# A chunk by seven block products in the first net too, and a turning without steps

## The chip, the cores and the metric

The kernel runs on one core of a Trainium2 chip. The metric is the device time of one execution in microseconds; the time before is the median of three runs. The span that the profile speaks of runs from the first to the last instruction of one profiled execution.

## The reference

Two layers, each of them a feed-forward net, a mixer (gated convolution, recurrence, pooling), cross attention to a memory, and a second feed-forward net, each followed by a residual and a layer norm. Everything is float32; x and mem are 256 x 1024. What the change touches is the net, which occurs four times (ffn1 and ffn2 of two layers), and the loading of the memory:

```python
D_MODEL = 1024; SEQ = 256; DEPTH = 2; N_MEM = 256; D_FF = 2816

def swiglu(x, w_gate, w_up, w_down):
    return (jax.nn.silu(x @ w_gate) * (x @ w_up)) @ w_down

def reference(x, mem, ...):
    h = x
    for l in range(DEPTH):
        h = layer_norm(ALPHA * h + 0.5 * swiglu(h, ffn1_gate[l], ffn1_up[l], ffn1_down[l]), ...)
        ...                                   # mixer, cross attention with mem
        h = layer_norm(ALPHA * h + 0.5 * swiglu(h, ffn2_gate[l], ffn2_up[l], ffn2_down[l]), ...)
    return h
```

## The kernel before

Every large product is done in three parts: each operand is split into a high part (a float32r copy, made by ScalarE, `whi`, `xTh`, `ah`) and a low part (the rest, a subtraction on VectorE, `wlo`, `xTl`, `al`), and `mm_rows` (L130) issues high x high, high x low and low x high into one PSUM tile. `split` (L60) makes both parts. So each weight that is loaded costs a copy on ScalarE and a subtraction on VectorE for every 128 x 1024 elements.

**Loading.** `load` (L64) brings weights in pieces of 1 MB into `raw` (three buffers) by a DMA on SP's queue, and splits each in two into `whi` and `wlo` (eight buffers each). A load waits until the buffer that it takes over has been split; a split waits until the products of the split eight before it are done.

**A net** (`ffn`, L376) goes over D_FF in chunks of 512 columns (five of them, and a last one of 256). For a chunk, `hidden` (L484) makes gate and up for all 256 tokens (2 weights x 2 token halves x 8 slices of D_MODEL x 3 parts = 96 products of 512 columns), `activate` (L401) and `gated` (L404) form silu(gate) * up in `sg`, and `turn` (L411) brings it to the layout with D_FF on the partitions: four DMAs deal `sg` out into `dealt`, VectorE turns it in 32 x 32 blocks (L418), and the result is split into `ah` and `al`. Down's products (`both`, L631; 24 of them for a slab of 256 rows) follow one chunk later: after chunk c come the second slab of chunk c-2 and the first of chunk c-1.

**A chunk by seven.** Three of the four nets make chunk 3 by `by_seven` (L515) in place of `hidden`. It takes gate and up as the two columns of a 2 x 2 block matrix (the rows being the halves of D_MODEL), x as 2 x 2 blocks (token half by half of D_MODEL), and forms the four result blocks from seven block products instead of eight, after Strassen and Winograd. Sums of x's blocks are made beforehand in `blocks_of_x` (L497: four sums of high and low parts, four combinations, four splits, kept in `kTh` and `kTl`). Sums of weight blocks are made on VectorE in the loaded tiles (L544), and each of the seven weight operands is split afresh: 14 splits. `put` (L565) combines the results. Its weight blocks lie in a tile `spare` (gate's upper half), in the tiles of the layer norm's parameters (`lng`, `lnb`: up's upper half) and in two of the three `raw` buffers.

**The first net** (`early` is set) does not: it also loads the memory (`load_memory`, L179; 32 DMAs on POOL's queue) and some small parameters, turns the memory on VectorE (L195) and splits it into `mTh` and `mTl`, behind chunk 2's work (L654 to L657).

**Order.** The kernel is written against a framework that plans the order of each engine's instructions when the program is built, from its own estimates; `issue_after` and `manual_schedule` steer it. On the chip each engine, and SP's queue of DMAs, then goes through its instructions strictly in that order, waiting at each for what it needs.

The lines that decide which net makes a chunk by seven, and where x's blocks are made:

```python
sevens = (3,) if early is None else ()
...
if c == 1 and sevens:
    bx = blocks_of_x()
```

Of the kernel before, what the change touches and what calls it, by code (L numbers as in the profile page):

```python
# [17 lines left out]
P = 128  # L18
# [28 lines left out]
def model(ctx: ExitStack, tc: tile.TileContext, t: dict, out: bass.AP):  # L47
# [16 lines left out]
    def load(src, k0, nk, c0, ncol, fine=False, strewn=False):  # L64

        hi, lo, todo = [], [], []
        step = 2048 // ncol
        for a in range(k0, k0 + nk, step):  # L70
            raw = wp.tile([P, 2048], F32, tag="raw", name="raw", bufs=3)
            raw = raw.rearrange("p (k c) -> p k c", c=ncol)
            half = step // 2
            part = 1 if fine else step
            for b in range(0, step, part):
                loads.append(nc.sync.dma_start(
                    raw[:, b : b + part, :],
                    src[:, c0 : c0 + ncol].rearrange("(p k) c -> p k c", p=P)[:, a + b : a + b + part, :]
                    if strewn
                    else src[(a + b) * P : (a + b + part) * P, c0 : c0 + ncol].rearrange("(k p) c -> p k c", p=P),  # L80
                ))
# [12 lines left out]
        return Weights(hi, lo, half, todo)  # L94
# [58 lines left out]

    jdn = cst.tile([P, P], F32, name="jdn")
# [24 lines left out]
    def load_memory(mp, behind):  # L179
        m = [mp.tile([P, 4, 8, 32], F32, tag="m", name="m", bufs=2) for _ in range(2)]  # L180
        with tc.issue_after(behind.ins):
            for n in range(2):
                for a in range(4):
                    for k in range(4):
                        c = (4 * n + k) * P + a * 32
                        nc.gpsimd.dma_start(
                            m[n][a * 32 : a * 32 + 32, k],
                            t["mem"][0, :, c : c + 32].rearrange("(b i) j -> i b j", i=32),
                        )

        def later():
            for n in range(2):
                for k in range(0, 4, 2):
                    turned = mp.tile([P, 2, SEQ], F32, tag="up", name="turned")
                    nc.vector.transpose(  # L195
                        turned.rearrange("p k t -> p (k t)"), m[n][:, k : k + 2].rearrange("p k b j -> p (k b j)")
                    )
# [6 lines left out]
    rows = cst.tile([P, P], F32, name="rows")  # L204
# [10 lines left out]
    def small_parameters(op):  # L215
        nc.gpsimd.memset(rows, 0.0)
# [13 lines left out]
        mf = op.tile([P, NT, len(narrow), 64], F32, name="mf", bufs=1)  # L230
# [61 lines left out]
    def finish(mm, y, scale, gb, last=False, flip=False):  # L292
# [6 lines left out]
        for i in range(NT):  # L299
# [8 lines left out]
            for c in pieces:  # L308
# [6 lines left out]
                else:  # L315
                    mm(
                        i, n, slice(0, 512), None,
                        None if last or not i or not n else lambda: transposed(h[0], 0, xTh, xTl),
# [21 lines left out]
        return lambda: transposed(h[1], 1, xTh, xTl, jdn if flip else idn)  # L340

    def project_back(slabs, late, gb, scale, between=lambda: None):
# [30 lines left out]
        return finish(tail, y, scale, gb)  # L373


    def ffn(l, name, n, pend=None, last=False, early=None):  # L376
        gate, up, down = (t[f"{name}_{x}"][l] for x in ("gate", "up", "down"))
        with tc.tile_pool(name="ffn", bufs=2, reuse_waits="tile") as fp:
# [21 lines left out]

            def activate(s, i, og):  # L401
                nc.scalar.activation(halves(s[:, i, :]), sums(og), AF.Silu)

            def gated(s, i, ou):  # L404
                v = halves(s[:, i, :])
                nc.vector.tensor_tensor(v, sums(ou), v, op=ALU.mult)
# [4 lines left out]
            def turn(s):  # L411
# [4 lines left out]
                for i in range(NT):  # L416
                    d = fp.tile([P, 4, P], F32, tag="up", name="square")
                    nc.vector.transpose(  # L418
                        d.rearrange("p k (i b) -> p b k i", b=4), x[:, :, i, :].rearrange("p b (j k) -> p b k j", k=4)
# [4 lines left out]
            def first():  # L424
# [5 lines left out]
                if pend is None:  # L430
# [8 lines left out]
                    with tc.manual_schedule(engines={E.Activation, E.DVE, E.PE}):  # L439
# [8 lines left out]
                        transposed_half(h[0], 0, 0, xTh, xTl)  # L448
                        busy(1)
                        split(*wg.todo[0])  # L450
                        transposed_half(h[0], 0, 1, xTh, xTl)
# [3 lines left out]
                        transposed_half(h[1], 1, 0, xTh, xTl)  # L455
                        group(1, 0)
                        split(*wg.todo[2])
                        transposed_half(h[1], 1, 1, xTh, xTl)
# [38 lines left out]
            def blocks_of_x():  # L497

                d = fp.tile([P, 4, 4 * P], F32, tag="spare", name="quarters", bufs=1)
                q = [d[:, n, :].rearrange("p (k t) -> p k t", t=P) for n in range(4)]  # L500
# [14 lines left out]
            def by_seven(c0, bx):  # L515
                def quarter(m, j, halves_of):
                    for b, r in enumerate(halves_of):
                        n = r.shape[1]
                        k = 4 * j + b * n
                        loads.append(nc.sync.dma_start(  # L520
                            r, m[k * P : (k + n) * P, c0 : c0 + CHUNK].rearrange("(k p) c -> p k c", p=P)
                        ))
                    return [r[:, 2 * h : 2 * h + 2, :] for h in range(2) for r in halves_of[:1]] if n == 4 else halves_of

# [3 lines left out]
                def raw():  # L528
                    return rows_by_columns(wp.tile([P, 2048], F32, tag="raw", name="raw", bufs=3))

                w00 = quarter(gate, 0, [rows_by_columns(
                    fp.tile([P, 4, 4 * P], F32, tag="spare", name="sum", bufs=1).rearrange("p n c -> p (n c)")
                )])
                w01 = quarter(up, 0, [
                    rows_by_columns(wp.tile([P, DM], F32, tag=g, name="raw")) for g in ("lng", "lnb")
                ])
                w11 = quarter(up, 1, [raw()])
                w10 = quarter(gate, 1, [raw()])

                def parts_of(r, plus=None):  # L540
                    hi, lo = [], []
                    for i in range(2):
# [4 lines left out]
                        h, w = (x.rearrange("p (k c) -> p k c", c=CHUNK) for x in (h, w))  # L547
# [14 lines left out]
                def half_sum():  # L562
                    return halves(fp.tile([P, 4, P], F32, tag="up", name="half").rearrange("p k t -> p (k t)"))

                def put(o, a, op, b):  # L565
                    nc.vector.tensor_tensor(o, a, b, op=op)

                s = activations()
                g = [halves(s[:, i, :]) for i in range(NT)]
                o = [acc((P, CHUNK)) for _ in range(4)]  # L570
                run(o[0], part_of_x(0, 0), parts_of(w00))
                nc.scalar.copy(g[0], sums(o[0]))
# [3 lines left out]
                put(e, sums(o[1]), ALU.add, g[0])  # L576
                run(o[3], bx[2], parts_of(w01, w11))
                put(g[1], sums(o[3]), ALU.add, e)
                f = half_sum()
                put(f, sums(o[2]), ALU.subtract, g[1])  # L580
                put(e, sums(o[2]), ALU.subtract, e)
                m = acc((P, CHUNK))
                run(m, part_of_x(0, 1), parts_of(w10))
                put(g[0], sums(m), ALU.add, g[0])
                nc.scalar.activation(g[0], g[0], AF.Silu)
                m = acc((P, CHUNK))
                run(m, part_of_x(1, 1), parts_of(w00, w10))
                put(g[1], sums(m), ALU.add, g[1])
                nc.scalar.activation(g[1], g[1], AF.Silu)
                put(g[1], g[1], ALU.mult, f)  # L590
                m = acc((P, CHUNK))
                run(m, bx[3], parts_of(w11))
                put(e, sums(m), ALU.add, e)
                put(g[0], g[0], ALU.mult, e)
                return turn(s)

            def last_hidden(c0):
# [11 lines left out]
                split(ah[:, 0:2, :], al[:, 0:2, :], s)  # L609
                return ah, al  # L610

            def slab(c, u):
                if c < len(chunks) - 1:
                    w = load(down[c * CHUNK : (c + 1) * CHUNK], 2 * u, 2, 0, DM, strewn=True)
                else:
                    w = load(down, c * 4, 2, 0, DM)
# [4 lines left out]
            sevens = (3,) if early is None else ()  # L621
# [17 lines left out]
            for c, (c0, ncol) in enumerate(chunks):  # L639
# [33 lines left out]
            return finish(tail, ys, 0.5, gb, last=last, flip=name == "ffn1")  # L673
# [27 lines left out]
    def mixer(l, fill):  # L701
        w_in = t["w_in"][l]
        with tc.tile_pool(name="mix", bufs=1, reuse_waits="tile") as mp:
# [284 lines left out]
            return project_back([slab(a) for a in (0, 6, 2, 4)], 3, gb, 1.0)  # L988


    def attention(l, pend):
        scale = (DM // HEADS) ** -0.5
        with tc.tile_pool(name="att", bufs=1, reuse_waits="tile") as ap:
# [108 lines left out]
            return project_back([slab(a) for a in (0, 2, 4, 6)], 3, gb, 1.0, others)  # L1102
# [40 lines left out]
```

## Time and profile before

| | |
|---|---|
| time, median of 3 runs | 1081.91 us (1081.46 to 1082.29) |
| the profiled execution | 1082.44 us, its span 1080.7 us |
| granted TensorE clock | 0.998 |
| PE (TensorE) busy | 1071.4 us, 99% of the span |
| DVE (VectorE) busy | 908.4 us, 84% |
| ACT (ScalarE) busy | 592.8 us, 55% |
| POOL (GpSimd) busy | 61.0 us, 6% |
| DMA | 231.86 MB, mean 215 GB/s |

In the profile's rows, an entry of the timeline is: start, duration, engine, line, operation, output <- inputs, shape, count, and in brackets the idle time just before it and what ended it. An entry of the chain of work that ended last is: start, duration, engine, output tile, line, count. A group's row ends with busy time and mean ns of one, and the idle time before them. The windows give for each stretch its length, then busy time and number of instructions of PE, of its weight loads, of DVE, ACT and POOL, the granted clock, the DMA engines' share and their GB/s. Instructions on an engine overlap a little, so that the step from one start to the next is shorter than the duration of one.

### The profile page before, as it was taken

Reading aid. Unit: us, or ns where it says so; the run is one execution under the profiler, and the core shown is the slowest. Engines: PE = TensorE matmul, PEld = TensorE weight load, DVE = VectorE, ACT = ScalarE, POOL = GpSimd, SP = SyncE. Lnnn points to the kernel's source line nnn. Section 1 sums busy time; section 2 is a strip of 40 time slices with the busy share of each in tenths; the row PEclk is TensorE's granted clock in tenths of the full one; section 3 lists DMA queues with packets and bytes.
Section 4 is the critical chain, followed back from the end, with each engine's and each line's share of the span. In section 5 each row is a group of like instructions: output and inputs, shape, how many; then the busy total and the mean of one; then the engine's idle time right before and its main releaser. Section 6 shows DMA issues by size and latency. Waiting matters only on the chain.

```text
span 1080.7 us, 15689 instructions
## 1 busy us (share of the span) xinstructions
PE 1071.4 (99%) x6015; PEld 947.5 (88%) x6015; DVE 908.4 (84%) x1198; ACT 592.8 (55%) x828; POOL 61.0 (6%) x113
## 2 busy tenths in 40 slices
PE   9999999999999999999999999999999999999997
PEld 7888888989899888888888888898898998888886
DVE  6678677998988898998697998798989889889885
ACT  6456553766457455556365465456764664645650
POOL 9500001000000000000000000010000000000000
PEclk9999999999999999999999999999999999999999
DMA  9986764754476387288468459656536664773761
GB/s 325 289 293 203 249 223 153 237 196 165 167 263 204 123 295 269 96 275 286 156 234 282 166 166 329 229 165 241 174 122 231 240 228 154 255 253 109 260 236 39
DMA packets 122715, 231.86 MB, mean 215 GB/s; under 512 B 6352, under 2 KB 45552, under 8 KB 117520
## 3 DMA queue, kind: packets, MB, share of 16 engines
q1 hardware_dynamic: 120848, 228.48, 63.1%
q0 software_dynamic: 1216, 1.20, 0.4%
q10 hardware_dynamic: 576, 1.18, 0.3%
q8 instruction: 47, 0.77, 0.3%
q14 instruction: 28, 0.23, 0.1%
HBM read 216.15 MB, written 1.05 MB: 201 GB/s over the span
## 4 chain that ended last, share of the span: by engine, by line
PE 99%; DMA 0%; DVE 0%; issue 0%; DVEq 0%
PE acc L106 65%; PE dn L106 30%; PE acc L170 1%; PE dn L845 1%; DMA h<-in_x_dram 0%; PE dn L904 0%; PE dn L903 0%; PE dn L893 0%; PE acc L969 0%; PE dn L810 0%; PE dn L437 0%; DVE h L334 0%; DVE h L330 0%; DVE st L322 0%; DVE h L314 0%
## 5 line engine op out<-in xcount | busy, mean ns | idle before, releaser
L62 DVE TENSOR_TENSOR wlo<-raw,whi 128x1024 fp32r<-128x1024 f32 (+1 forms) x390 | 460.8, 1207 | 91.0 <-ACT whi L61 81.1
L61 ACT CAST whi<-raw 128x1024 fp32r<-128x1024 f32 (+1 forms) x390 | 391.2, 1040 | 258.3 <-PE dn L106 128.4
L106 PE MATMUL acc<-whi,xT 128*128 128x512 f32 x1192 | 359.7, 380 | 0.0
L106 PEld LDWEIGHTS acc<-whi,xT 128*128 128x128 f32 x1192 | 225.2, 189 | 32.1
L106 PE MATMUL acc<-wlo,xT 128*128 128x512 f32 x596 | 225.9, 379 | 0.0
L106 PE MATMUL acc<-xT,whi 128*128 128x512 f32 x576 | 142.1, 382 | 0.0
L106 PE MATMUL dn<-whi,ah 128*128 128x512 f32 x346 | 131.5, 380 | 0.0
L106 PE MATMUL dn<-wlo,ah 128*128 128x512 f32 x346 | 131.2, 379 | 0.0
L106 PE MATMUL dn<-whi,al 128*128 128x512 f32 x346 | 131.1, 379 | 0.0
L106 PEld LDWEIGHTS acc<-wlo,xT 128*128 128x128 f32 x596 | 112.7, 189 | 15.7
L106 PEld LDWEIGHTS acc<-xT,whi 128*128 128x128 f32 x576 | 104.1, 190 | 11.8
L106 PE MATMUL dn<-whi,xT 128*128 128x512 f32 x288 | 88.8, 382 | 0.0
L106 PEld LDWEIGHTS acc<-xT,wlo 128*128 128x128 f32 x576 | 75.5, 191 | 3.9
L106 PE MATMUL acc<-xT,wlo 128*128 128x256 f32 x576 | 75.9, 275 | 0.0
L106 PEld LDWEIGHTS dn<-wlo,ah 128*128 128x128 f32 x346 | 65.4, 189 | 9.5 <-DVE wlo L62 0.3
L106 PEld LDWEIGHTS dn<-whi,al 128*128 128x128 f32 x346 | 65.4, 189 | 9.3
L106 PEld LDWEIGHTS dn<-whi,ah 128*128 128x128 f32 x346 | 65.4, 189 | 9.1
L418 DVE STREAM_TRANSPOSE square<-dealt 128x512 f32<-128x512 f32 x40 | 62.8, 1645 | 3.8 <-DMA dealt<-sg 3.8
L327 POOL TENSOR_TENSOR rs<-rs,nhalf 128x1 f32<-128x1 f32 x16 | 14.9, 928 | 846.3 <-DVE rs L326 846.3
L106 PEld LDWEIGHTS dn<-whi,xT 128*128 128x128 f32 x288 | 54.7, 190 | 7.8 <-DVE xT L62 0.3
L106 PE MATMUL dn<-wlo,xT 128*128 128x512 f32 x144 | 54.8, 381 | 0.0
L61 ACT CAST ah<-square 128x512 fp32r<-128x512 f32 x40 | 24.6, 619 | 39.7 <-DVE square L418 39.7
(227 smaller groups left out, 1174.0 us busy)
## 6 DMA issues: line engine op xcount, KB each, us to landing
raw<-in_ffn_down_dram SPq DMA_DIRECT2D x44, 1024.0 KB, 5.4
raw<-in_ffn_up_dram SPq DMA_DIRECT2D x41, 1024.0 KB, 6.1
raw<-in_ffn_gate_dram SPq DMA_DIRECT2D x39, 1024.0 KB, 5.1
raw<-in_w_in_dram SPq DMA_DIRECT2D x24, 1024.0 KB, 5.0
dealt<-sg SPq DMA_DIRECT2D x80, 128.0 KB, 3.8
raw<-in_ca_k_dram SPq DMA_DIRECT2D x8, 1024.0 KB, 4.9
raw<-in_w_out_dram SPq DMA_DIRECT2D x8, 1024.0 KB, 4.8
raw<-in_ca_v_dram SPq DMA_DIRECT2D x8, 1024.0 KB, 5.4
```

What stands on the lines that cost most here:

```text
L61: nc.scalar.copy(hi, src)
L62: lows.append(nc.vector.tensor_tensor(lo, src, hi.bitcast(F32), op=ALU.subtract))
L106: nc.tensor.matmul(o, w, x, start=start, stop=stop)
L170: nc.tensor.transpose(pt[:, k, :], src[:, (4 * j + k) * P : (4 * j + k + 1) * P], unit)
L327: nc.gpsimd.tensor_tensor(rs, rs, nhalf[:, 0:1], op=ALU.pow)
L418: nc.vector.transpose(d.rearrange("p k (i b) -> p b k i", b=4), x[:, :, i, :].rearrange("p b (j k) -> p b k j", k=4))
L845: nc.tensor.matmul(o[g, hh, :], kc[:, hh, g], x, start=True, stop=True)
```

## The change

1. The first net makes chunk 4 by seven (`sevens = (4,)`). Its `blocks_of_x` is called after the memory's turning has been issued, with c = 2; the layer norm's parameters are loaded only at c = 5, since their tiles hold weight blocks until then.
2. The weight blocks get other tiles. `spare` becomes three tiles of 512 KB. In the first net gate's upper half lies in a whole `raw` buffer, up's lower half in another, gate's lower half in `spare0` and `spare1` (which before that hold the memory and x's blocks); in the other nets gate's upper half in `spare0` and `spare1`, gate's lower half in `dealt` and `spare2`, up's lower half in a `raw` buffer. Every block is loaded by two DMAs of 512 KB.
3. In `by_seven` the product with up's lower half moves ahead of the two with gate's lower half, and the final silu and product go into a second `sg` tile.
4. The turning: `activate` and `gated` write their columns in another order, in two pieces of 256 per token half, and `turn` reads and writes runs of 32 elements in place of steps of four. Down's rows are then loaded in their natural order, the tokens stand in another order in x's layout (a permuted identity `pdn` in the transposes on TensorE for the nets), and the last chunk's activations are split in that order.

Cut to its core, the diff is:

```diff
+    pdn = cst.tile([P, P], F32, name="pdn")
+    nc.gpsimd.tensor_copy(pdn.rearrange("p (r b) -> p b r", b=4), idn.rearrange("p (b r) -> p b r", b=4))
...
     def load_memory(mp, behind):
-        m = [mp.tile([P, 4, 8, 32], F32, tag="m", name="m", bufs=2) for _ in range(2)]
+        m = [
+            mp.tile([P, DM], F32, tag=f"spare{n}", name="m", bufs=1).rearrange("p (k b j) -> p k b j", k=4, j=32)
+            for n in range(2)
+        ]
...
+            def ordered(v):
+                return v.rearrange("p (a k j) -> p k a j", a=4, j=32)
+
+            def by_two(v, o):
+                o = o.rearrange("p (n a j m) -> p m n a j", n=2, a=4, m=2)
+                return [(ordered(v)[:, 2 * m : 2 * m + 2], o[:, m]) for m in range(2)]
+
             def activate(s, i, og):
-                nc.scalar.activation(halves(s[:, i, :]), sums(og), AF.Silu)
+                for v, o in by_two(s[:, i, :], og):
+                    nc.scalar.activation(v, o, AF.Silu)

             def gated(s, i, ou):
-                v = halves(s[:, i, :])
-                nc.vector.tensor_tensor(v, sums(ou), v, op=ALU.mult)
+                for v, o in by_two(s[:, i, :], ou):
+                    nc.vector.tensor_tensor(v, o, v, op=ALU.mult)
...
                     nc.vector.transpose(
-                        d.rearrange("p k (i b) -> p b k i", b=4), x[:, :, i, :].rearrange("p b (j k) -> p b k j", k=4)
+                        d.rearrange("p k (b r) -> p b k r", b=4), x[:, :, i, :].rearrange("p b (k j) -> p b k j", k=4)
                     )
...
             def blocks_of_x():
-                d = fp.tile([P, 4, 4 * P], F32, tag="spare", name="quarters", bufs=1)
+                d = [fp.tile([P, DM], F32, tag=f"spare{n}", name="quarters", bufs=1) for n in range(2)]
...
             def by_seven(c0, bx):
...
-                w00 = quarter(gate, 0, [rows_by_columns(fp.tile([P, 4, 4 * P], F32, tag="spare", ...))])
-                w01 = quarter(up, 0, [rows_by_columns(wp.tile([P, DM], F32, tag=g, ...)) for g in ("lng", "lnb")])
-                w11 = quarter(up, 1, [raw()])
-                w10 = quarter(gate, 1, [raw()])
+                w00 = block(gate, 0, pieces("spare0", "spare1") if early is None else whole())
+                w01 = block(up, 0, pieces("lng", "lnb"))
+                w11 = block(up, 1, whole())
+                w10 = block(gate, 1, pieces("dealt", "spare2") if early is None else pieces("spare0", "spare1"))
...
                 put(e, o[2], ALU.subtract, e)
+                o = [acc((P, CHUNK)) for _ in range(3)]
+                run(o[0], bx[3], parts_of(w11))
+                put(e, o[0], ALU.add, e)
+                run(o[1], part_of_x(0, 1), parts_of(w10))
+                put(g[0], o[1], ALU.add, g[0])
+                run(o[2], part_of_x(1, 1), parts_of(w00, w10))
+                put(g[1], o[2], ALU.add, g[1])
+                s = fp.tile([P, NT, CHUNK], F32, tag="spare2", name="sg", bufs=1)
+                for i, u in enumerate((e, f)):
+                    v = ordered(s[:, i, :])
+                    nc.scalar.activation(v, g[i].rearrange(...), AF.Silu)
+                    nc.vector.tensor_tensor(v, v, u.rearrange(...), op=ALU.mult)
                 return turn(s)
...
-            sevens = (3,) if early is None else ()
+            sevens = (3,) if early is None else (4,)
...
-                if c == 1 and sevens:
+                if sevens and c == 1 and early is None:
                     bx = blocks_of_x()
                 if c == (max(sevens) + 1 if sevens else 1):
-                    with tc.issue_after(loads[-1].ins) if early is not None else nullcontext():
-                        gb = ln_params(l, n)
-                        rest = early(fp) if early is not None else ()
+                    gb = ln_params(l, n)
+                if c == 1 and early is not None:
+                    with tc.issue_after(loads[-1].ins):
+                        rest = early(fp)
                 if c == 2 and early is not None:
                     with tc.issue_after(lows[-1].ins):
                         for f in rest:
                             f()
+                    if sevens:
+                        bx = blocks_of_x()
```

More of the change, by code (lines that the diff above doesn't have):

```diff
@@ L317, in finish @@
                         i, n, slice(0, 512), None,
-                        None if last or not i or not n else lambda: transposed(h[0], 0, xTh, xTl),
+                        None if last or not i or not n else lambda: transposed(h[0], 0, xTh, xTl, units[0]),
                     )
@@ L515, in by_seven, with whole, pieces, block @@
             def by_seven(c0, bx):
[L516 to L523, printed above, removed]
                 def rows_by_columns(r):
                     return r.rearrange("p (k c) -> p k c", c=CHUNK)
[L528 to L536, printed above, removed]
-                w11 = quarter(up, 1, [raw()])
-                w10 = quarter(gate, 1, [raw()])
+                def whole():
+                    r = rows_by_columns(wp.tile([P, 2048], F32, tag="raw", name="raw", bufs=3))
+                    return [r[:, 0:2, :], r[:, 2:4, :]]
+                def pieces(*tags):
+                    pools = {"lng": wp, "lnb": wp}
+                    return [
+                        rows_by_columns(pools.get(g, fp).tile([P, DM], F32, tag=g, name="raw", bufs=1)) for g in tags
+                    ]
+                def block(m, j, to):
+                    for i in range(2):
+                        k = 4 * j + 2 * i
+                        loads.append(nc.sync.dma_start(
+                            to[i], m[k * P : (k + 2) * P, c0 : c0 + CHUNK].rearrange("(k p) c -> p k c", p=P)
+                        ))
+                    return to
+                w00 = block(gate, 0, pieces("spare0", "spare1") if early is None else whole())
+                w01 = block(up, 0, pieces("lng", "lnb"))
+                w11 = block(up, 1, whole())
+                w10 = block(gate, 1, pieces("dealt", "spare2") if early is None else pieces("spare0", "spare1"))
                 def parts_of(r, plus=None):
@@ L671, in tail @@
                         rows_of(a, i, k, m, first, u == 2 and k == 1, cols, alone)
[L673 removed]
+            return finish(tail, ys, 0.5, gb, (idn, jdn) if name == "ffn1" else (pdn, pdn), last=last)
     def keys(l, c, between={}):
```

77 lines of the change are left out of this document (33 added, 44 removed).

## Prediction

> **What bounds the kernel now.** I read the page's first part, then the chain of work that ended last in order of time, then the windows and the timeline of VectorE around the stretches that the diff touches.
>
> ```profile
> span 1080.7 us, 15689 instructions
> PE 1071.4 (99%) x6015; PEld 947.5 (88%) x6015; DVE 908.4 (84%) x1198; ACT 592.8 (55%) x828; POOL 61.0 (6%) x113
> 19.78 31.08 PE acc L106 x144
> ...
> 87.23 20.72 PE acc L106 x96
> 107.95 10.36 PE dn L106 x48
> 118.31 20.72 PE acc L106 x96
> 139.03 10.36 PE dn L106 x48
> ...
> 450.92 18.13 PE acc L106 x84
> ...
> 639.45 10.56 PE dn L106 x48
> ```
>
> TensorE is the bound: the chain is matmuls nearly from end to end. 20.72 / 96 = 0.2158 us from one 512-column product to the next, and 84 x 0.2158 = 18.13: the chunk by seven in the second net runs without a gap. The one excess I see is 0.20 us at 639.45. So only two things count: fewer matmuls, and whether TensorE still finds its operands.
>
> **Part by part: the products.** The plain chunk at 118.31 (the fifth, c = 4) has 96 products; by seven it has 7 x 4 x 3 = 84. 12 x 0.2158 = 2.59 us go, all on the path. Everything else in the diff is off the path as long as it arrives in time.
>
> **The feeding of that chunk.** A product needs the weight's high part (ScalarE) and low part (VectorE). A chunk by seven needs 14 splits in place of 8, 8 sums of weight blocks, 7 combinations of results, and x's four blocks (12 operations) beforehand.
>
> ```profile
> core 0: us, PE busy (x) PEld busy (x) DVE busy (x) ACT busy (x) POOL busy (x), PEclk, DMA share, GB/s
> 86.00:108.00 22.00, 22.00 (x103) 19.27 (x102) 21.09 (x37) 16.07 (x20) 0.00 (x0) 1.00 0.53 185
> 110.00:150.00 40.00, 40.00 (x187) 35.04 (x186) 26.18 (x24) 18.59 (x21) 0.00 (x0) 1.00 0.73 238
> 440.00:480.00 40.00, 40.00 (x187) 35.04 (x186) 39.29 (x41) 22.28 (x25) 0.00 (x0) 1.00 0.49 156
> ```
>
> Where a chunk is made by seven today (440 to 480) VectorE works 39.29 of 40 us. In the first net it has room from 110 to 150 (26.18), but none just before: from 86 to 108, where the memory is turned, 21.09 of 22. The change queues x's blocks exactly there. What today's chunk by seven has that the new one lacks is a head start:
>
> ```profile
> 433.95 1.23 DVE L62 TENSOR_TENSOR wlo<-sum,whi 128x1024 fp32r<-128x1024 f32 x1 [0.93 <-ACT whi L61]
> ...
> 440.01 0.68 DVE L406 TENSOR_TENSOR sg<-acc,sg 128x512 f32<-128x512 f32 x1
> 440.61 1.22 DVE L62 TENSOR_TENSOR wlo<-sum,whi 128x1024 fp32r<-128x1024 f32 x1
> 441.74 0.68 DVE L406 TENSOR_TENSOR sg<-acc,sg 128x512 f32<-128x512 f32 x1
> 442.34 1.22 DVE L62 TENSOR_TENSOR wlo<-sum,whi 128x1024 fp32r<-128x1024 f32 x1
> 443.48 2.35 DVE L544 TENSOR_TENSOR sum<-sum,raw 128x1024 f32<-128x1024 f32 x2
> 445.75 1.22 DVE L544 TENSOR_TENSOR raw<-raw 128x1024 f32<-128x1024 f32 x1
> ...
> 455.51 1.27 DVE L62 TENSOR_TENSOR al<-square,ah 128x512 fp32r<-128x512 f32 x2
> 456.71 3.48 DVE L62 TENSOR_TENSOR wlo<-raw,whi 128x1024 fp32r<-128x1024 f32 x3
> ...
> 468.78 1.20 DVE L62 TENSOR_TENSOR wlo<-raw,whi 128x1024 fp32r<-128x1024 f32 x1
> ```
>
> Splits for the chunk that starts at 450.92 begin at 433.95, before the previous chunk's L406 has its results (440.01, 441.74); in today's order three splits and three sums stand ahead of the second L406. Even so the lead is small: the split of 468.78 ends at 469.98 and its product stands at about 470.4. In the changed program's instruction order the first net's DVE queue holds, after the memory's turning: x's blocks between four down splits, then the four halves of the previous chunk's gating, and only behind them the first of the fourteen splits. The engine runs in order, so no part of that work starts before the previous chunk's last product, 107.95.
>
> **The sum on VectorE.** Start to start a 128x1024 operation takes (445.75 - 443.48) / 2 = 1.135 us and a 128x512 one (456.71 - 455.51) / 2 = 0.60.
>
> ```profile
> 86.20 3.17 DVE L418 STREAM_TRANSPOSE square<-dealt 128x512 f32<-128x512 f32 x2 [1.74 <-DMA dealt<-sg]
> 89.26 1.17 DVE L62 TENSOR_TENSOR wlo<-raw,whi 128x1024 fp32r<-128x1024 f32 x1
> 90.36 1.27 DVE L62 TENSOR_TENSOR al<-square,ah 128x512 fp32r<-128x512 f32 x2
> 91.56 0.17 DVE L260 COPY prm<-acc 128x32 f32<-128x32 f32 x1
> ...
> 92.01 0.69 DVE L195 STREAM_TRANSPOSE turned<-m 128x512 f32<-128x512 f32 x1
> ...
> L418 DVE STREAM_TRANSPOSE square<-dealt 128x512 f32<-128x512 f32 x40 | 62.8, 1645 | 3.8 <-DMA dealt<-sg 3.8
> L1054 DVE STREAM_TRANSPOSE square<-dealt 128x512 f32<-128x512 f32 x6 | 4.2, 705 | 0.0
> L127 DVE TENSOR_TENSOR sums<-acc,sums 128x256 f32<-128x256 f32 x32 | 13.3, 419 | 2.5 <-ACT sums L126 2.5
> ```
>
> The turning without steps has no row of its own; its ends are L418 (1645 ns, steps of four on both sides) and L1054 (705 ns, runs of 32, the shape that the new one has). I take L1054's, 0.62 start to start: 0.87 saved on each. A gating half is bounded by L127 (419 ns): 0.34 start to start.
>
> From 86.20, in the new order: 2 turnings (1.25), 6 splits (6.8), 2 splits of the activations (1.2), the memory's 4 turnings (2.5) and 4 splits (2.4), fifteen small ones at (92.01 - 91.56) / 4 = 0.11 (1.7), x's 12 (7.2): 23.1, so to 109.3, then 4 gating halves (1.4): 110.7. From there to the last of the fourteen splits: 14 splits and 8 sums, 22 x 1.135 = 25.0, and eleven of 0.60 (two turnings, two activation splits, six combinations, one product of silu), 6.6: 142.3. TensorE wants that split after 13 x 6 products and one more: 118.31 + 79 x 0.2158 = 135.4. Two down products stand ahead of it in the new order (0.43). TensorE loses 142.3 - 135.8 = 6.5 us, in several waits.
>
> **Behind it, one more wait.** In the first net the block that is added to (w00) lies in one of the three raw buffers until that last sum is split. The next down load but one needs that buffer, and stands in SP's queue behind the previous chunk's dealing and the norm's two loads, ahead of the sixth chunk's gate and up loads.
>
> ```profile
> raw<-in_ffn_down_dram SPq DMA_DIRECT2D x44, 1024.0 KB, 5.4
> 117.10 1.06 ACT L61 CAST whi<-raw 128x1024 fp32r<-128x1024 f32 x1 [2.88 <-DVE square L418]
> ```
>
> 142.3 + 5.4 + 1.06 = 148.8 for its high part, 149.9 for the low one. TensorE has 5 products of the chunk and 22 down ones left, 27 x 0.2158 = 5.8, and stands there at 148.1: waits of 0.7 and 0.9, and some 0.2 at the second half. I take 1.8. After that the loads follow close on each other, and VectorE is back in its 26 of 40 us.
>
> Sum: -2.59 + 6.5 + 1.8 = +5.7. The profiled execution took 1082.44 (span 1080.7 and 1.74 around it), 0.5 above the median of 1081.91; on the median it gives 1087.6. Bounds: if VectorE is free at 107.95, 1.7 less, and a landing of 4.4 in place of 5.4 takes off 1.0: +3.0, 1084.9. If the turning stays at L418's price, two pairs lie in the sum above: 4 x 0.87 = +3.5, 1091.1.
>
> [...]
>
> **What I cost at nothing.** In the other three nets the split order keeps the early start (three splits ahead of the gating), and the turning inside the stretch is 2 x 0.87 shorter: the 0.4 us lead grows. Splitting activations and gating in two adds 0.34 x 2 - 0.60 = 0.08 on VectorE each, hidden by the same. The permuted identity is one more POOL copy, and the order of tokens changes no matmul. The last chunk's activations are split in two pieces with steps, four times in all, where VectorE has room; down's rows are loaded as w_out's are today. The blocks' loads now come as 512 KB pairs.
>
> ```profile
> 7.05 5.98 SPq L76 DMA_DIRECT2D raw<-in_ffn_up_dram  x2
> 17.60 1.99 ACT L61 CAST whi<-raw 128x1024 fp32r<-128x1024 f32 x2 [0.87 <-DMA raw<-in_ffn_up_dram]
> 18.69 2.40 DVE L62 TENSOR_TENSOR wlo<-raw,whi 128x1024 fp32r<-128x1024 f32 x2 [0.47 <-ACT whi L61]
> 5.00:10.00 5.00, 5.00 (x22) 4.15 (x21) 2.57 (x4) 2.69 (x6) 4.80 (x11) 1.00 1.05 388
> 10.00:15.00 5.00, 5.00 (x26) 4.23 (x25) 4.87 (x8) 4.04 (x9) 5.00 (x11) 1.00 1.02 337
> ```
>
> One of them moves far: up's block of the fifth chunk (lng, lnb) is issued between the first chunk's two up loads, where the DMA engines are full. 1 MB at 388 to 337 GB/s delays the second up load by 2.7 to 3.1 us. Its first low part is ready at 18.69 + 1.2 = 19.9 and wanted at 19.78 + 25 x 0.2158 = 25.2: 5.3 of cover, 2.2 left. If that cover were gone, the delay would be paid in full.
>
> **Rivals.** (a) VectorE keeps up and only the 2.59 count: 1079.3. It decides if the chain above is 7 us shorter, that is, if the splits start before 107.95. For it: today's three chunks by seven lose nothing. Against: the order. 7%. (b) The starvation is there but half as long, because combinations and products overlap better than I count: 1081.91 - 2.59 + 4.2 = 1083.5. 10%. (c) The start starves as well, by the full 3.1 us: 1090.7. 5%. (d) The clock falls in the starved stretch:
>
> ```profile
> 7.03 0.85 PE dn L437 x2
> ```
>
> at the start two products take 0.85, half speed. If the 27 products behind the longest wait ran so, that is 5.8 more: 1093.4. 4%, since the waits come in pieces of about 2 us with products between. [...] (e) My forecast: 74%.
>
> **Numbers.** 1087.6. The range takes in (b)'s upper part, the bounds and (c): 1083.9 to 1091.1; (a) and (d) are left out. No change means within 0.2%, 2.2 us, about what a measurement of this kernel can tell: faster is (a), 0.07; same is the lower part of (b), 0.06; slower 0.87.
>
> **What would show it.** Right: 84 products in the first net's fifth chunk, with waits of PE on wlo and whi of 5 to 9 us in all between about 128 and 150; VectorE without idle from 90 to 150; first split after both gatings; a down load issued only behind the last sum. Turning rows near 705 ns. The other nets' chunks by seven at 18.13. Wrong: an unbroken 18.13 there, or waits before 30 us.

## The result, and the profile after

The changed kernel takes 1087.2 us, the median of four runs (1086.23 to 1087.89), against 1081.68 before: a ratio of 1.0049, 95% interval 1.0032 to 1.0067. Six more runs of it, made beside the experiments, gave 1087.88 and a ratio of 1.0057 (1.0044 to 1.0069). It is slower, by what was forecast to within half a microsecond. The time was lost where the prediction put it, but one term of the sum did not occur, and several smaller losses that the sum did not have came in its place.

The profiled execution took 1086.68 us, its span 1084.9. First the chain of work that ended last, in order of time (start, duration, engine, output tile, line, count; the product line L106 is now L103, the sums of weight blocks L544 are L562, the combinations in `put` are L584, the gating L406 is L420, the turning L418 is L433):

```profile
19.22 31.08 PE acc L103 x144
...
86.67 20.72 PE acc L103 x96
107.39 10.36 PE dn L103 x48
117.75 6.42 PE acc L103 x30
124.18 1.14 DVE wlo L62
125.31 2.27 DVE raw L562 x2
127.58 0.60 DVE half L584
128.18 1.15 DVE wlo L62
...
129.37 8.23 PE acc L103 x29
...
138.31 1.14 DVE raw L562
...
140.51 1.05 ACT whi L61
...
141.60 0.70 PE dn L103 x2
142.30 1.08 PE acc L103 x5
143.38 9.93 PE dn L103 x46
...
163.79 18.37 PE dn L103 x84
...
455.07 18.13 PE acc L103 x84
```

But for one hole, this is TensorE nearly from end to end, as before. The first net's fifth chunk begins at 117.75. Its 84 products and the two down products among them would take 86 x 0.2158 = 18.56 and end at 136.31; the remaining 46 down products begin at 143.38. That is 7.07 us of starvation. From 124.18 to 129.33, and again from 137.62 until ScalarE's last copies, the chain runs over VectorE: splits, sums of weight blocks, combinations. The 8.23 us of TensorE between them are 29 products, which would take 29 x 0.2158 = 6.26; the granted clock had fallen there (see rival (d) below). In the other nets the chunk by seven still takes 18.13.

VectorE's timeline there (start, duration, engine, line, operation, output <- inputs, shapes, count, idle time before it and what ended that):

```profile
107.29 0.68 DVE L62 TENSOR_TENSOR kTl<-quarters,kTh 128x512 fp32r<-128x512 f32 x1
107.89 1.41 DVE L420 TENSOR_TENSOR sg<-acc,sg 128x256 f32<-128x256 f32 x4
109.22 2.35 DVE L62 TENSOR_TENSOR wlo<-raw,whi 128x1024 fp32r<-128x1024 f32 x2
111.49 3.49 DVE L562 TENSOR_TENSOR raw<-raw 128x1024 f32<-128x1024 f32 x3
...
137.62 0.69 DVE L584 TENSOR_TENSOR sg<-acc,sg 128x512 f32<-128x512 f32 x1 [0.24 <-PE acc L103]
...
140.63 3.50 DVE L62 TENSOR_TENSOR wlo<-raw,whi 128x1024 fp32r<-128x1024 f32 x3 [0.59 <-ACT whi L61]
```

The last of x's blocks is split just before the four gating halves (L420), and the first of the chunk's fourteen splits starts at 109.22, behind them. The windows say the same:

```profile
core 0: us, PE busy (x) PEld busy (x) DVE busy (x) ACT busy (x) POOL busy (x), PEclk, DMA share, GB/s
86.00:108.00 22.00, 22.00 (x104) 19.26 (x103) 21.51 (x44) 16.77 (x25) 0.00 (x0) 1.00 0.44 152
108.00:142.00 34.00, 30.14 (x127) 24.44 (x126) 33.17 (x38) 15.53 (x18) 0.00 (x0) 0.95 0.43 129
```

VectorE is busy for 33.17 of 34 us while TensorE falls to 30.14 and ScalarE to 15.53. ScalarE is named by some of TensorE's waits (acc waits 3.1 us for whi), but it has half of that stretch free: it waits for VectorE's sums itself, 13.3 us in four waits of `whi` on `raw`.

### The profile page after: what moved, and what is told of

It reads as the page before. It is cut to its first block, busy times and chain, and to the rows that moved or that the text cites. A ratio compares the mean times of both kernels' runs of the same rounds, so it can differ in the third digit from the quotient of the medians.

```text
span 1084.9 us, 15815 instructions
## 1 busy us (share of the span) xinstructions
PE 1071.5 (99%) x6003; PEld 945.5 (87%) x6003; DVE 906.4 (84%) x1267; ACT 606.8 (56%) x875; POOL 62.3 (6%) x114
## 4 chain that ended last, share of the span: by engine, by line
PE 98%; DVE 1%; DMA 0%; issue 0%; ACT 0%; DVEq 0%; SPq 0%; ACTq 0%
PE acc L103 65%; PE dn L103 30%; PE acc L170 1%; PE dn L866 1%; DMA raw<-in_ffn_gate_dram 0%; PE dn L925 0%; DVE raw L562 0%; DVE wlo L62 0%; PE dn L914 0%; PE dn L924 0%; ACT whi L61 0%; PE acc L990 0%; PE dn L831 0%; DVE h L338 0%; DVE h L334 0%
## 5 line engine op out<-in xcount | busy, mean ns | idle before, releaser
L62 DVE TENSOR_TENSOR wlo<-raw,whi 128x1024 fp32r<-128x1024 f32 (+1 forms) x420 | 496.6, 1208 | 105.5 <-ACT whi L61 96.8
L61 ACT CAST whi<-raw 128x1024 fp32r<-128x1024 f32 (+1 forms) x420 | 421.4, 1042 | 277.4 <-PE dn L103 114.1
L103 PE MATMUL acc<-whi,xT 128*128 128x512 f32 x1152 | 348.7, 380 | 1.9 <-ACT whi L61 1.9
L103 PEld LDWEIGHTS acc<-whi,xT 128*128 128x128 f32 x1152 | 217.7, 189 | 33.2 <-ACT whi L61 2.3
L103 PE MATMUL acc<-wlo,xT 128*128 128x512 f32 x576 | 218.4, 379 | 0.0
L103 PE MATMUL acc<-xT,whi 128*128 128x512 f32 x576 | 142.1, 382 | 0.0
L103 PE MATMUL dn<-whi,ah 128*128 128x512 f32 x346 | 131.4, 380 | 0.5 <-ACT whi L61 0.5
L103 PE MATMUL dn<-wlo,ah 128*128 128x512 f32 x346 | 131.2, 379 | 0.0
L103 PE MATMUL dn<-whi,al 128*128 128x512 f32 x346 | 131.1, 379 | 0.0
L103 PEld LDWEIGHTS acc<-wlo,xT 128*128 128x128 f32 x576 | 108.9, 189 | 15.5 <-DVE wlo L62 0.3
L103 PEld LDWEIGHTS acc<-xT,whi 128*128 128x128 f32 x576 | 104.1, 190 | 11.8
L103 PE MATMUL dn<-whi,xT 128*128 128x512 f32 x288 | 88.3, 381 | 0.0
L103 PEld LDWEIGHTS acc<-xT,wlo 128*128 128x128 f32 x576 | 75.5, 191 | 3.9
L103 PE MATMUL acc<-xT,wlo 128*128 128x256 f32 x576 | 75.9, 275 | 0.0
L103 PEld LDWEIGHTS dn<-whi,ah 128*128 128x128 f32 x346 | 65.3, 189 | 9.9 <-ACT whi L61 0.8
L103 PEld LDWEIGHTS dn<-wlo,ah 128*128 128x128 f32 x346 | 65.4, 189 | 9.7 <-DVE wlo L62 0.4
L103 PEld LDWEIGHTS dn<-whi,al 128*128 128x128 f32 x346 | 65.4, 189 | 9.2
L103 PEld LDWEIGHTS dn<-whi,xT 128*128 128x128 f32 x288 | 54.4, 189 | 7.6 <-DVE xT L62 0.2
L103 PE MATMUL dn<-wlo,xT 128*128 128x512 f32 x144 | 54.8, 380 | 0.0
L324 DVE SCALAR_TENSOR_TENSOR h<-h,dn 128x512 f32<-128x512 f32 x31 | 21.1, 682 | 27.3 <-PE dn L103 27.3
L103 PE MATMUL acc<-whi,mT 128*128 128x512 f32 x128 | 40.2, 380 | 0.0
```

Of the source, the lines that this page charges most:

```text
L61: nc.scalar.copy(hi, src)
L62: lows.append(nc.vector.tensor_tensor(lo, src, hi.bitcast(F32), op=ALU.subtract))
L103: nc.tensor.matmul(o, w, x, start=start, stop=stop)
L324: nc.vector.scalar_tensor_tensor(v, v, ALPHA / scale, sums(y[i][n]), op0=ALU.mult, op1=ALU.add)
```

## The experiments

The theory after the result: VectorE, in order and without idle time from 87 us on, is the bound of the first net's chunk; x's blocks beside the memory's turning take the time in which the chunk's splits would have run ahead. The rivals: something else of the change costs (the turning, the tiles, the loads), ScalarE or the loads are what is late, or the clock.

**Only the first net back to plain chunks.**

```diff
-            sevens = (3,) if early is None else (4,)
+            sevens = (3,) if early is None else ()
```

> The changed kernel, but the first net makes all its chunks plainly again: the turning without steps, the other tiles and the other three nets' sevens stay. VectorE's lateness in the first net's seven-product chunk as the whole loss: 1081.1 us (1080.4 to 1081.9), as before less the 0.56 us by which the chunk begins earlier. If the turning, the tiles or the other nets cost: 1084 to 1087.

Measured: 1081.51 us, ratio 1.0001 (0.9992 to 1.0010). Together, the turning, the tiles and the other nets' new order cost and bring nothing; the whole loss is the one chunk. The 0.56 us of earlier start that the expectation counted as a gain was none: the profiled execution of before had a span of 1080.7, while most of its other runs (1079.7 to 1080.5) and this kernel have 1079.8.

**x's blocks earlier.** They are made with c = 1, in the two tiles `lng` and `lnb` that are free then.

```diff
             def blocks_of_x():
-                d = [fp.tile([P, DM], F32, tag=f"spare{n}", ...) for n in range(2)]
+                d = [fp.tile(... tag=f"spare{n}" ...) if early is None else wp.tile(... tag=("lng", "lnb")[n] ...) for n in range(2)]
...
-                if sevens and c == 1 and early is None:
-                    bx = blocks_of_x()
+                if sevens and c == 1:
+                    with tc.issue_after(loads[-1].ins) if early is not None else nullcontext():
+                        bx = blocks_of_x()
...
-                    if sevens:
-                        bx = blocks_of_x()
```

> x's blocks of the first net are made behind its second chunk, in the two normalization tiles, and not beside the memory's turning; nothing else is moved by hand. VectorE's queue ahead of the chunk as the cause: 12 instructions, 7.2 us, leave the stretch from 86 us on, VectorE's last split falls from 142 to about 135 us, which is when TensorE wants it; 1078.3 to 1079.8 us, faster than both kernels. If VectorE's work within the chunk (38 us by its own rows) is the cause and not what stands ahead: 1083 to 1086. If ScalarE's roundings or the loads are what is late: 1086 to 1087, as the changed kernel.

Measured: 1079.55 us (1079.48 to 1081.05), ratio 0.9982 (0.9974 to 0.9991). This version beats both kernels, and in its chain the chunk by seven is unbroken:

```profile
117.63 18.13 PE acc L103 x84
```

With the blocks gone the planner filled the place with the chunk's own work, as VectorE's timeline shows:

```profile
102.44 2.49 DVE L567 TENSOR_TENSOR raw<-raw 128x1024 f32<-128x1024 f32 x2
104.84 1.22 DVE L62 TENSOR_TENSOR wlo<-raw,whi 128x1024 fp32r<-128x1024 f32 x1
106.10 1.23 DVE L567 TENSOR_TENSOR raw<-raw 128x1024 f32<-128x1024 f32 x1
107.24 0.75 DVE L420 TENSOR_TENSOR sg<-acc,sg 128x256 f32<-128x256 f32 x2
```

Sums of weight blocks (L567 here) now stand ahead of the gating. Its windows show how near the edge it is: TensorE whole, VectorE 37.56 of 38.

```profile
86.00:108.00 22.00, 22.00 (x104) 19.26 (x103) 20.97 (x39) 16.09 (x23) 0.00 (x0) 1.00 0.68 232
108.00:146.00 38.00, 38.00 (x178) 33.28 (x177) 37.56 (x41) 22.96 (x26) 0.00 (x0) 1.00 0.55 167
```

**No sums of weight blocks in the first net.**

```diff
-                        if plus is not None:
+                        if plus is not None and early is None:
                             nc.vector.tensor_tensor(r[i], r[i], plus[i], op=ALU.add)
```

> The changed kernel without the eight sums of weight blocks in the first net's chunk (left out; the seven products use the blocks unsummed). VectorE as the bound: 8 times 1.14 = 9.1 us less in the chunk, last split at 133 us, ahead of TensorE's want: 1078.3 to 1079.8 us. If ScalarE's roundings or the loads are late, of which nothing is taken away: 1085 to 1087. If the clock's fall makes the loss: 1083 to 1085.

Measured: 1079.24 us, ratio 0.9980 (0.9971 to 0.9989). This kernel leaves the sums out of what it computes, and nothing else. Taking work from VectorE alone, with every copy of ScalarE's and every load kept, removes the whole loss. ScalarE and the loads fall as rivals. So does the clock: with the splits held behind the gating and with the steps back (both below) the loss stands, and the profiled clock is 1.00 throughout the chunk.

**x's blocks twice over.** The call of `blocks_of_x` for the first net is repeated.

> The changed kernel, x's blocks of the first net made twice over: 12 instructions, 7.2 us, more for VectorE in the stretch in which it has no idle time. VectorE as the bound of that stretch: 7.2 us longer, and up to 2 more where the last chunk's loads come late behind it: 1094.4 to 1096.5. If TensorE, ScalarE or the loads share the bound there, less than 5 us: under 1092.

Measured: 1096.68 us (1095.33 to 1100.32), ratio 1.0143 (1.0128 to 1.0158): 9 us more than the changed kernel for 7.2 us more of VectorE, shortest against shortest (1095.33 and 1086.23); the median lies just above the range that was expected. The profiled run, the longest, is no measure of the blocks alone. It lost 4.7 us before they were made: its chain has the 96 products that start at 55.48 in the changed kernel at 60.16, behind loads that took longer to land (up's 1 MB from 10 to 52 us 9.6 us in the median, in the changed kernel 7.2). And its granted clock was 0.87 from 108 to 142 us:

```profile
133.00:143.00 10.00, 8.47 (x19) 5.77 (x19) 9.45 (x9) 7.67 (x8) 0.00 (x0) 0.50 0.19 68
```

**The order alone.** Two kernels that differ in one thing. In both, x's blocks are queued behind the second chunk's last split; in the second, each split of the chunk is also queued behind the gating.

```diff
-                    with tc.issue_after(loads[-1].ins) if early is not None else nullcontext():
+                    with tc.issue_after(lows[-1].ins) if early is not None else nullcontext():
                         bx = blocks_of_x()
```

> As with x's blocks early, but held behind the last split of the second chunk, so that all twelve instructions lie between 65 and 87 us, still ahead of the memory's turning. VectorE's work ahead of the chunk as the cause: that they leave the stretch from 87 us on decides and not where they go, 1079.0 to 1079.8 us. If their place in VectorE's early gaps mattered: 1081 to 1083.

```diff
+                    gates.append(nc.vector.tensor_tensor(v, o, v, op=ALU.mult))
...
-                        split(h, w, r[i])
+                        with tc.issue_after(gates[-1].ins) if early is not None else nullcontext():
+                            split(h, w, r[i])
```

> The kernel with x's blocks held behind the second chunk's last split, and in the first net's seven-product chunk each split queued behind the previous chunk's four gating halves, as the changed kernel has them. The amount of work is that of the faster kernel, the order that of the slower. If the order is half of the cause: VectorE idles from about 102 us (86.2 plus 23.1 less 7.2) until the gating's product at 107.4, some 5.3 us, less the splits of the down block that may go ahead, 3.4; 2 to 5 us lost: 1081.5 to 1084.5. If the amount alone decides: 1079.0 to 1079.8. If the order alone decides: 1086 to 1087.

Measured: 1081.31 us (1079.54 to 1083.45; ratio 0.9995, 0.9986 to 1.0003) and 1086.77 us (1084.95 to 1087.44; ratio 1.0042, 1.0030 to 1.0055). The first missed its expectation: where the blocks go does matter, by 1.8 us in the median. Put in one lump they delay the third chunk's gating and with it the dealing and the loads; in its chain a load of up's block stands at 100.58 for 4.70 us. VectorE's turning there starts at 87.25 after 3.51 us of waiting for the dealing, where with the blocks early it was 84.64 and 0.93. The second lost more than expected. Its VectorE:

```profile
89.37 1.30 DVE L433 STREAM_TRANSPOSE square<-dealt 128x512 f32<-128x512 f32 x2 [5.43 <-DMA dealt<-sg]
...
101.41 3.57 DVE L62 TENSOR_TENSOR wlo<-raw,whi 128x1024 fp32r<-128x1024 f32 x3
106.01 0.76 DVE L420 TENSOR_TENSOR sg<-acc,sg 128x256 f32<-128x256 f32 x2 [1.03 <-PE acc L103]
107.31 0.76 DVE L420 TENSOR_TENSOR sg<-acc,sg 128x256 f32<-128x256 f32 x2 [0.54 <-PE acc L103]
107.98 2.35 DVE L62 TENSOR_TENSOR wlo<-raw,whi 128x1024 fp32r<-128x1024 f32 x2
```

VectorE stands idle in front of the gating with splits behind it, and the first one starts at 107.98, hardly earlier than the changed kernel's 109.22. Part of the time that the blocks left went idle sooner, in the 5.43 us of waiting for the dealing. That wait is 1.9 us longer than in the first kernel's profile, ahead of the place where the two differ; but since VectorE still waits for TensorE's products at the gating (1.03 and 0.54 us), it is not what held the chunk's splits up. The order costs 5.5 us between the medians of these two. So both halves are needed: the blocks must leave, and the time that they leave must be filled with the chunk's work.

**x's sums on GpSimd.** In `blocks_of_x`, `nc.gpsimd.tensor_tensor` in place of `nc.vector.tensor_tensor` in the first net.

> The changed kernel, the eight sums and differences of x's blocks of the first net made by GpSimd, which is idle from 50 us on; their four splits stay on VectorE, and the planner then puts splits and sums of the chunk ahead of two of the gating halves. VectorE's work ahead of the chunk and its order as the cause: 8 times 0.6 = 4.8 us less, filled with the chunk's own splits, last split at 137.5 instead of 142.3 us where TensorE wants it at 136; 1080.5 to 1082.5 us. If freed time is not filled, as where the splits stand behind the gating: 1084 to 1086. If GpSimd is late with them or slows VectorE: 1087 or more.

Measured: 1089.33 us, ratio 1.0071 (1.0057 to 1.0084), no faster than the changed kernel and in the median slower (the intervals overlap), although the planner ordered the chunk's splits ahead of the gating. VectorE's timeline while GpSimd works:

```profile
90.70 3.41 DVE L62 TENSOR_TENSOR wlo<-raw,whi 128x1024 fp32r<-128x1024 f32 x2
94.03 1.23 DVE L277 TENSOR_TENSOR s<-e 128x4 f32<-128x4 f32 x1
...
103.08 4.51 DVE L62 TENSOR_TENSOR wlo<-raw,whi 128x1024 fp32r<-128x1024 f32 x2
```

and the groups of GpSimd (name, shapes, count, busy us, mean ns):

```profile
L518 POOL TENSOR_TENSOR quarters<-xT 128x512 f32<-128x512 f32 x4 | 7.8, 1955 | 42.9 <-DVE turned L198 40.8 <-DVE lbs L283 2.1
```

Two splits take 3.41 and 4.51 us where two take 2.35 without GpSimd, and an operation of 4 columns takes 1.23. VectorE's busy time from 86 to 108 us was 21.66 us with 32 instructions, against 21.51 with 44 in the changed kernel: what was moved away came back as longer instructions. What holds VectorE up there the trace does not name.

GpSimd was late as well. The chain runs over its sums, and the last one stands there at 106.58:

```profile
99.14 3.47 POOL quarters L518 x2
...
106.58 2.15 POOL quarters L526
```

ScalarE's copy of that sum, at 108.76, has the last three pieces of the gating's silu behind it, and the gating on VectorE starts at 116.86 in place of 107.89. How much each of the two costs was not separated.

**The turning in steps again**, in the changed kernel and in the faster one.

```diff
-                        d.rearrange("p k (b r) -> p b k r", b=4), x[:, :, i, :].rearrange("p b (k j) -> p b k j", k=4)
+                        d.rearrange("p k (i b) -> p b k i", b=4), x[:, :, i, :].rearrange("p b (j k) -> p b k j", k=4)
```

> The changed kernel, its turning of a chunk read and written in steps again (this leaves the columns of a chunk in another order, so the order is what is left out). VectorE late in one chunk of the first net only: the two turnings in the stretch without idle cost 0.94 us more each, 1.9 in all: 1089.1 us (1088.3 to 1090.3); the other nets' turnings cost nothing. If the turning has no part in it: 1087.2. If every net pays: over 1092.

> The kernel with x's blocks behind the second chunk and each chunk's turning in steps again (which leaves the columns of a chunk in another order). VectorE at its edge in every net's seven-product chunk: the first net, full from 87 to 146 us but for 1.1 us, loses 1 to 3 us, the three others 1.3 each as they did with the steps in the changed kernel: 1084.5 to 1086.5 us. If the steps cost only where VectorE is already late: 1079.5 to 1080.5.

Measured: 1094.43 us (ratio 1.0117, 1.0103 to 1.0131) and 1085.38 us (ratio 1.0039, 1.0026 to 1.0051). The rows of the turning, in the changed kernel and then with steps:

```profile
L433 DVE STREAM_TRANSPOSE square<-dealt 128x512 f32<-128x512 f32 x40 | 26.0, 687 | 1.5 <-DMA dealt<-sg 1.5
```

```profile
L433 DVE STREAM_TRANSPOSE square<-dealt 128x512 f32<-128x512 f32 x40 | 62.7, 1646 | 7.3 <-DMA dealt<-sg 7.2
```

The first expectation missed, by 5 us, and its rival, that every net pays, came true. Set mark against mark along the two chains, the first net loses 2.9 us (1.9 were expected), and each of the three others 1.4, which I had held to be free. In the faster kernel the three lose 1.35 each again and the first net 1.8, which was foretold once the first miss was known. So the turning without steps gives no time of its own, but all four chunks by seven stand on it in this order of instructions: in the three other nets two turnings in the stretch are 1.9 us, and only some 0.5 of that was spare.

**Two chunks by seven in each of the other nets**, on top of the blocks behind the second chunk:

```diff
-            sevens = (3,) if early is None else (4,)
+            sevens = (2, 4) if early is None else (4,)
```

> As with x's blocks held behind the second chunk's last split, and the other three nets make two chunks each, the third and the fifth, by seven products. TensorE alone: 36 products fewer, 7.8 us, 1071.5 us. With VectorE as the second bound: one such chunk keeps it busy for 26.5 of 28 us and the stretch ahead of it for 26.4 of 31, and in these nets the third chunk comes right behind the making of x's blocks, so that it starves as the first net's did, 4 to 7 us in each net: 1083 to 1093.

Measured: 1099.30 us, ratio 1.0169 (1.0154 to 1.0184). TensorE has 36 products fewer and the kernel is 18 us slower than the one it builds on: VectorE is busy for 61.83 of 63 us from 378 to 441, and the waits come in all three nets: 0.8 to 1.2 us in the third chunk (437.66 in the second net), and 3.1 to 3.5 us in the fifth (498.43 to 503.18 there). The direction was foretold, the size was not.

## Why the prediction was right, point by point

- **The products.** 84 in the chunk, 2.59 us fewer on TensorE: the chain of the kernel with early blocks has the chunk in an unbroken 18.13, and its span is 2.3 us shorter than the plain one's (1079.8 to 1077.5; the time 1.96, 1081.51 to 1079.55). Right.
- **VectorE is late because the splits stand behind gating and blocks.** Right in mechanism and nearly in its marks: first split 109.22 (predicted 110.7); the last is the first of the three that start at 140.63 and ends at about 141.8 (142.3); starvation 7.07 (6.5). The queue ahead was ready 1.4 us sooner than summed, 1.0 of it since the stretch's first turning ran at 83.75 and not at 86.20; two waits of VectorE, 0.24 and 0.59, gave part of that back. One sign came out smaller than named: the waits that the profile names for TensorE from 127 to 142 us are 3.86 us in all (0.76, 0.46, 0.31, 1.87, 0.46) and not 5 to 9. The rest of the 7.07 is TensorE at the lower clock, 1.7, and the slower start of products behind each wait (the first takes 0.48 us, where the step from one to the next is 0.2158).
- **"Behind it, one more wait", 1.8 us.** This step failed. SP's queue:

```profile
131.61 0.38 SPq L75 DMA_DIRECT2D raw<-in_ffn_down_dram  x1
141.89 0.38 SPq L75 DMA_DIRECT2D raw<-in_ffn_gate_dram  x1
```

  The down load went out at 131.61, before the last sum (138.31 in the chain); it took over another raw buffer. The load that waited for the summed block's buffer is the next chunk's gate (141.89, as that block's last split ends), whose products come 46 down products later. Behind 143.38 the chain has 0.24 us too much (18.37 at 163.79). I had not followed which of the three buffers each load takes. With the stepped turning such a wait does appear: there the chain stands for 8.31 us on a load of the sixth chunk's up block that starts at 146.25.
- **The sum.** 7.07 - 2.59 = 4.48, 0.16 by a later start than in the plain kernel (19.22 against 19.06) and 0.24 behind it: 4.88 of the 5.1 by which this span exceeds 1079.8. So the forecast +5.7 met the measured +5.5 of the medians in part by luck. The 1.8 did not occur; 0.6 more of starvation, the 0.16 and the 0.24 made up for half of it in this execution; in the other traced one the clock added 1.7, next.
- **Rival (d), the clock.** It was given 4% and held unlikely since the waits would come in pieces of about 2 us. That such waits leave the clock whole was an estimate of mine; here it fell behind waits of 0.76 us and less. The row at 7.03 from which the half speed was taken shows no fall: the granted clock there is 1.00 (7.03 to 7.88 us in the profile of before). TensorE's timeline, and a window of the same stretch:

```profile
126.49 0.38 PE L103 MATMUL acc<-whi,kTl 128*128 128x512 f32 x1
127.63 0.48 PE L103 MATMUL acc<-whi,kTh 128*128 128x512 f32 x1 [0.76 <-ACT whi L61]
128.58 0.48 PE L103 MATMUL acc<-whi,kTh 128*128 128x512 f32 x1 [0.46 <-ACT whi L61]
129.37 0.48 PE L103 MATMUL acc<-wlo,kTh 128*128 128x512 f32 x1 [0.31 <-DVE wlo L62]
...
131.14 0.63 PE L103 MATMUL acc<-whi,xT 128*128 128x512 f32 x1
131.56 0.63 PE L103 MATMUL acc<-wlo,kTh 128*128 128x512 f32 x1
...
131.00:133.00 2.00, 2.00 (x6) 1.55 (x6) 2.00 (x3) 1.32 (x2) 0.00 (x0) 0.50 0.70 193
```

  Three waits under a microsecond with two products between them, three more products at full speed, and then eight that stand 0.43 us apart, until 133.3. In this execution that cost next to nothing: VectorE was the bound, and waited 0.24 us for a product. In the profiled execution of the second set the clock held through that stretch and fell behind the last waits, 1.54 and 0.46 us:

```profile
141.00:143.00 2.00, 1.96 (x7) 1.61 (x8) 0.72 0.21 24
143.00:145.00 2.00, 2.00 (x6) 1.64 (x5) 0.50 1.00 341
145.00:147.00 2.00, 2.00 (x10) 1.69 (x10) 0.93 1.09 387
```

  (PE, its weight loads, the clock, the DMA engines' share, GB/s.) There TensorE is the bound again, and from 141.04 on it took 1.7 us more than the first execution for the same products; that run took 1087.95 us. So the ten runs' scatter, 1086.2 to 1089.4, may be in part where the clock falls; I have that from two traces only. The second set was made to see whether the runs with the lower mean clock are the longer ones. The two shortest of the ten do have the highest (0.999 and 0.998), but the other eight, 1086.68 to 1089.37, all show 0.996 or 0.997, so that it is not shown. Nor do the traces show what makes the clock fall. The price of (d), 5.8 us, was too high for these two executions: in both the clock was at half for 3.4 us, which is 1.7 us of lost work. That is no limit: with the blocks made twice the clock stayed at half for 10.2 us, from 133.0 to 143.2.
- **Rivals (a), (b), (c).** (a) and (b) fell by the 7.07. (c): TensorE has no wait between the start and 124 us, so the hoisted load stayed inside its cover.
- **What was costed at nothing.** That the other nets lose nothing is right (18.13 in each). That their lead grows by the shorter turning is not: with the steps back they lose 1.4 us each, where the kernel before, with the same steps, lost nothing. The new order or the new tiles must use up most of what the turning gives; which of them was not tried.

## What to carry to other kernels

Before giving TensorE less work by giving another engine more, look at that engine's queue just ahead of the place: a stretch with 21 of 22 us busy has no room for 7 us, even if the next 40 us have 14 to spare. Room was used here only where the work that is wanted next stood ahead of the instruction that waits; freeing time in front of such a wait without moving work into it gained 0.4 us between the medians (1086.77 against 1087.20). And a load's buffer has to be followed by name through the rotation before a wait on it is put into a sum.

## What the runs showed of the hardware

- VectorE was held up while GpSimd made 128x512 sums at 1.96 us each: two 128x1024 splits took 3.41 and 4.51 us in place of 2.35, and a sum of 4 columns 1.23 in place of 0.15, so 1.1 us more, or twice that.
- The granted clock fell to half after 2.9 us in which TensorE began only two products, with no wait above 0.76 us, and came back after 3.4 us; with the blocks made twice it was down for 10.2 us. The length of one wait did not decide it: with the splits held behind the gating waits of up to 1.0 us left it whole (1.00 from 118 to 150 us), and with the sums on GpSimd even one of 2.87 us (before the product at 130.86; 1.00 from 108 to 142 us).
- Three kernels spend 2.0 to 2.1 us of their time outside the span: blocks early (1079.55 with 1077.5), early with the steps, and behind the second chunk's last split. All others spend 1.7 to 1.8 (1079.24 with 1077.5 for the one without sums), also the two others that make the blocks there, with the splits behind the gating and with two chunks by seven. What that is stays open.
